# VectorE's order in the late position steps of a Fourier-mixing encoder: lower parts ahead of the late sum and the norm

## The chip, the core and the metric

One NeuronCore of a Trainium2 chip runs the whole program. TensorE (PE in the profile, with its weight loads as PEld) multiplies matrices into PSUM, VectorE (DVE) and ScalarE (ACT) work element by element, GpSimd (POOL) does small things and some transfers, SyncE (SP) issues most transfers. Each engine runs its own instructions strictly in the order in which they were written for it and waits on semaphores for the others. The metric is the device time of one execution in microseconds, the median of several runs.

## The reference

Two sequences (2048 and 512 positions, 1024 channels) pass an attention layer and a Fourier-mixing layer, each with a gate and a residual, and a final RMSNorm. The change lies in the Fourier layer's tail:

```python
def fourier_layer(x, g, w_gate, w_out):
    h = rmsnorm(x, g)
    hg = h.astype(jnp.float32).reshape(b, s, N_FGROUPS, FGROUP_CH)
    f = jnp.fft.fftn(hg, axes=(1, 3), norm="ortho").real
    gate = h @ w_gate
    return x + (f * jax.nn.silu(gate)) @ w_out
# trunk: ... return rmsnorm(x, final_norm)
```

## The kernel before

Float32 products are made of three TensorE products of a high and a lower part ("fp32r"): ScalarE casts a tile to its high part, VectorE subtracts that from the tile to get the lower part, and `matmul3` (L117) issues high x high, high x lower, lower x high. So of every three matmuls the second needs VectorE's lower part.

The transform over the 2048 positions is split by 16: after butterflies on VectorE (`pm`, L1261) there are nine position transforms k1 = 0 to 8. Transform k1 multiplies the tables of sines and cosines with a real and an imaginary tile, in two halves of 512 columns: `halves_of` (L1394) makes the parts, called gp_half_i (i = 0 real, 1 imaginary), and `position` (L1412) the products ABp_0 and ABp_1 (12 + 12 matmuls). VectorE then combines ABp into two row tiles `up` (L1445 to L1448), multiplies them by the gates s2p (L1451), TensorE transposes them (`tw`, L95), and the output product with w_out follows. The transforms come in the order 0, 8, 4, 2, 6 and then, in a loop of **late steps**, 1, 7, 3, 5. The inputs of 7, 3 and 5 are written to DRAM when the butterflies make them (`god`, on ACT's queue, L1824) and read back later (`go`, on SP's queue, L1841). In the text "step 7" is the late step that transforms k1 = 7; while it does so, TensorE also makes the output product of the transform before (k1 = 1).

From transform 6 on the output product is done by `Outs.products` (L1565) with seven 512 x 512 products for two row tiles xa and xb, by sums of operands (a Winograd scheme). In PE's order:

- W = A00 x wo, then VectorE adds W to xa: the **first sum**;
- Z = S1 x T1, then VectorE adds Z to the upper half of xb: the **Z add**. Z is not cleared: the S4 product below accumulates on it, so PE must wait for the Z add;
- ABp_0 of the next transform, W += S2 x T2 (PE must wait for the first sum), ABp_1;
- Z += S4 x wo, then X, half of W += S3 x T3, the transposes `tw`, the other half, the next step's A00, seven matmuls of its Z, then W += A11 x N4 of this step, and the **late sum** (VectorE adds W to the lower half of xb);
- then the **norm** of xb: squares on ScalarE (jkf, L1056), mean (invf, L110), the power on GpSimd (L111), the scaling on VectorE (L1468), a store of the row tile (L1470).

What is late in one step (late sum, norm of xb, third sum S3 and tT_11 of `rest`) is written into the next step, among the parts of the next transform. `seq("dve", ...)` chains VectorE's instructions of these steps in the order in which the Python code calls them, so the code's order is the engine's order; PE's, ACT's and SP's places are left to a scheduler that follows. The hooks are `split_g` (L1849, called after the first sum), `transform` (L1865) and `turns` (L1871). Before, VectorE's order in `split_g` and `transform` is: late sum, first sum, real lower part, mean of the norm, imaginary lower part, S3, tT_11, scaling, Z add, then both lower parts of the second half.

Of the kernel before, what the change touches and what calls it, by code (L numbers as in the profile page):

```python
# [42 lines left out]
def encoder(  # L43
# [120 lines left out]
    def seq(engine, ins):  # L164

        after(ins, chain.get(engine))
        chain[engine] = ins
        return ins
# [822 lines left out]
    def fourier_phase(tail):  # L991
        with ExitStack() as es:
# [401 lines left out]
            def halves_of(name, gr, gs, hf, after_one=None):  # L1394

                out = []
                for i, g in enumerate((gr, gs)):
                    if i and after_one:
                        after_one()
                    if g is not None:  # L1400
                        t = main.tile([P, 2, 512], F32R, align_bytes=LINE, tag="hT", bufs=8, name=f"g{name}_{hf}_{i}")
                        gv = g[:, hf * 512 : hf * 512 + 512]
                        ACT.copy(t[:, 0], gv)
                        low = DVE.tensor_tensor(t[:, 1], gv, f32(t[:, 0]), ALU.subtract)
                        if chain.get("steps"):
                            seq("dve", low)
                        out.append(t)
                return out
# [65 lines left out]
            def normed(x2, r):  # L1474
                norm(x2, r)()
# [8 lines left out]
            def finish(uT, r, between=None):  # L1484
                r0 = r[0]
                x2 = residual(r)
                for half in range(2):
                    if half and between:
                        chain["turns"] = end
                        between()  # L1490
                    ps = psum2.tile([P, 512], F32, tag="acc", name=f"fo{r0}_{half}")
                    for k in range(KD):
                        first_one = k == 0 and half == (between is not None)
                        end = matmul3(
                            ps, uT[k], wo[half * KD + k], k == 0, k == KD - 1, behind=chain.get("turns") if first_one else None
                        )
                    xs = x2[:, half * 512 : half * 512 + 512]
                    DVE.tensor_tensor(xs, xs, ps, ALU.add)
                if between:
                    late[0] = x2, r  # L1500
                else:
                    normed(x2, r)
                return end
# [3 lines left out]
            class Outs:  # L1507
# [57 lines left out]
                def products(self, hooks, last=False):  # L1565
# [5 lines left out]
                    def add(t, half, ps):  # L1571
                        return DVE.tensor_tensor(t[:, q[half]], t[:, q[half]], ps, ALU.add)
# [41 lines left out]
                        upper()  # L1614
                    if not last:
                        prod(W, A[1, 1], ft["N4"], four, False)
                        seq("dve", add(xb, 0, W))
                        return xb, self.us[1][1]
                    ss = main.tile([P, 8], F32, tag="ss", bufs=2, name="ssl")
                    junk = fp.tile([P, 512], F32, tag="c12", bufs=1, name="jkl").bitcast(BF16)  # L1620

# [142 lines left out]
            def pm(a, b, name):  # L1764

                n = zt(name)
                tt(n, a, b, A)
                tt(a, a, b, S)
                return n, a
# [45 lines left out]
            o0s, o1s = pm(tsn[1], tsn[3], "o0s")  # L1815
            g1r, g7r = pm(e0c, o0c, "g1r")
            g1s, g7s = pm(o0s, e0s, "g1s")
            g3r, g5r = pm(e1c, o1s, "g3r")
            p6 = [halves_of("p6", *G[6], 0), None]
            g5s, g3s = pm(o1c, e1s, "g5s")  # L1820
            G[1], G[7], G[3], G[5] = (g1r, g1s), (g7r, g7s), (g3r, g3s), (g5r, g5s)
            for k1 in (7, 3, 5):
# [22 lines left out]
            for k1, k2 in ((1, 7), (7, 3), (3, 5), (5, None)):  # L1845
                name, tiles = f"p{k1}", pair(k1, 16, 0)
                gl, tb = nxt["r"]

                def split_g():  # L1849

                    nxt["s"] = [gated(name, r, place) for r, place in zip(tiles, (xtile, left))]
                    scaled = []

                    def weigh():
                        if late[0]:
                            scaled.append(norm(*late[0], "dve"))

                    nxt["p"] = [halves_of(name, *gl, 0, weigh), None]
                    o.rest()
                    for f in scaled:  # L1860
                        f()
                    if not ft["T3"]:
                        f_sums("T3", right)

                def transform(third):  # L1865
                    if not ft["N4"]:
                        f_sums("N4", left)
                    nxt["p"][1] = halves_of(name, *gl, 1)
                    nxt["o"] = Outs(k1, position(name, k1, *gl, tiles, (nxt["s"], tb), nxt["p"], third))

                def turns():  # L1871
                    nxt["o"].operands()
                    nxt["o"].load()
                    if k2:
                        nxt["r"] = reads(k2)

                late[0] = o.products((split_g, transform, turns, lambda: nxt["o"].others()))
                o = nxt["o"]
            o.products((lambda: (o.rest(), normed(*late[0])), lambda third: third(), lambda: None), last=True)


    fourier_phase(attention_phase())
# [98 lines left out]
```

## Time and profile before

| what | value |
|---|---|
| median of 3 runs | 1584.42 us (1582.39 to 1585.3) |
| the profiled execution | 1583.8 us, of which the profile's span is 1582.0 |
| granted TensorE clock | 0.999 of full speed |
| busy share of the span | PE 99%, PEld 83%, DVE 73%, ACT 56%, POOL 28% |
| transform 6 and late steps 1, 7, 3, 5 | about 1428 to 1561 us of the span |

In the profile a row of the timeline reads: start in us from the span's start, length in us, engine, line, operation, output <- inputs, shape, how many were merged, and in brackets the idle time before it with what ended that. A matmul's length includes its passage through the array, so the next may start before it ends; the distance of two starts is what a matmul costs. VectorE's lengths overlap a little in the same way (a 128x512 subtraction is 0.69 long, and the next instruction starts 0.60 after it).

### The profile page before, as it was taken

How to read it: one execution, taken by the hardware profiler on the slowest of the kernel's cores; microseconds unless marked ns; L12 is line 12 of the kernel's file. 1: busy time of each engine (PE TensorE's matmuls, PEld its weight loads, DVE VectorE, ACT ScalarE, POOL GpSimd, SP SyncE). 2: the span in 40 equal slices, each digit the busy share in tenths (PEclk: the TensorE clock that was granted, in tenths of full speed). 3: DMA queues.
4: the chain of work that ended last, by engine and by line, in shares of the span. 5: the costliest groups of instructions: out<-in, count | busy, mean ns of one | idle time of the engine just before them, and what ended most of it. 6: DMA issues, size and time to landing. Idle time of an engine off the chain costs nothing.

```text
span 1582.0 us, 27728 instructions
## 1 busy us (share of the span) xinstructions
PE 1568.8 (99%) x9882; PEld 1315.8 (83%) x9882; DVE 1151.3 (73%) x2793; ACT 878.1 (56%) x2096; POOL 444.2 (28%) x614
## 2 busy tenths in 40 slices
PE   9999999999999999999999999999999999999998
PEld 7888888888888888988888888888888888887776
DVE  6888556877457886378764577669778878988886
ACT  7788535776246784267751576546555554343343
POOL 2475642421404314024222242223112121111110
PEclk9999999999999999999999999999999999999999
DMA  8597686575856567665659566675557569448752
GB/s 302 205 331 280 227 356 210 210 266 194 303 202 225 207 234 271 214 221 210 251 172 326 205 231 231 236 259 196 191 213 253 180 228 411 171 181 313 278 180 81
DMA packets 100997, 373.91 MB, mean 236 GB/s; under 512 B 11267, under 2 KB 22283, under 8 KB 83452
## 3 DMA queue, kind: packets, MB, share of 16 engines
q1 hardware_dynamic: 83148, 298.17, 52.9%
q0 software_dynamic: 16400, 70.04, 11.4%
q10 hardware_dynamic: 1312, 3.94, 0.7%
q8 instruction: 78, 1.28, 0.3%
q14 instruction: 59, 0.48, 0.1%
HBM read 280.84 MB, written 91.26 MB: 235 GB/s over the span
## 4 chain that ended last, share of the span: by engine, by line
PE 91%; DVE 4%; DMA 2%; ACT 1%; issue 1%; POOL 0%; POOLq 0%; SPq 0%; DVEq 0%; ACTq 0%
PE gp L117 14%; PE qp L117 14%; PE spt L117 11%; PE op L117 7%; PE W L117 7%; PE av L615 6%; PE spt L530 6%; PE fo L117 4%; PE vp L117 3%; PE Z L117 3%; PE pt L589 3%; PE Wo L117 2%; PE z L117 2%; PE X L117 2%; PE ABp L117 1%; PE Zo L117 1%
## 5 line engine op out<-in xcount | busy, mean ns | idle before, releaser
L117 PE MATMUL gp<-h,wg 128*128 128x512 f32 x960 | 237.7, 396 | 0.0
L117 PE MATMUL qp<-h,wq 128*128 128x512 f32 x960 | 237.1, 396 | 0.0
L549 DVE CUSTOM_DVE_ANT_0 S<-spt,b 128x385 f32<-128x385 f32 (+1 forms) x320 | 156.6, 528 | 105.7 <-PE spt L530 68.4
L117 PEld LDWEIGHTS gp<-h,wg 128*128 128x128 f32 x960 | 174.9, 188 | 37.2 <-issue 1.0
L117 PEld LDWEIGHTS qp<-h,wq 128*128 128x128 f32 x960 | 174.9, 188 | 36.6 <-issue 0.2
L557 ACT ACTIVATE S<-S 128x385 f32<-128x385 f32 (+1 forms) x320 | 188.8, 597 | 19.6 <-DVE S L549 19.3
L597 ACT CAST pts<-pt 128x384 fp32r<-128x384 f32 (+1 forms) x240 | 100.5, 457 | 167.6 <-PE pt L589 158.4
L598 DVE TENSOR_TENSOR pts<-pt,pts 128x384 fp32r<-128x384 f32 (+1 forms) x240 | 114.3, 520 | 23.7 <-ACT pts L597 22.7
L117 PE MATMUL spt<-wo,uT 128*128 128x512 f32 x480 | 120.3, 391 | 0.0
L639 POOL TENSOR_TENSOR uT<-o,uT 128x256 fp32r<-128x256 f32 x75 | 55.5, 740 | 229.8 <-ACT uT L638 229.7
L117 PE MATMUL op<-wo,uT 128*128 128x512 f32 x480 | 118.9, 391 | 0.0
L530 PE MATMUL spt<-kwin,qab 64*128 64x384 f32 (+1 forms) x960 | 118.5, 353 | 0.0
L615 PEld LDWEIGHTS av<-pts,v 128*128 128x128 f32 x576 | 101.4, 188 | 18.8
L615 PE MATMUL av<-pts,v 128*128 128x512 f32 (+1 forms) x576 | 115.7, 341 | 0.0
L117 PE MATMUL fo<-wo,tTu 128*128 128x512 f32 x480 | 115.5, 392 | 0.0
L117 PEld LDWEIGHTS op<-wo,uT 128*128 128x128 f32 x480 | 89.4, 188 | 18.5
L117 PEld LDWEIGHTS spt<-wo,uT 128*128 128x128 f32 x480 | 89.1, 188 | 18.3
L117 PEld LDWEIGHTS fo<-wo,tTu 128*128 128x128 f32 x480 | 88.3, 188 | 17.5 <-ACT wo L1722 0.3
L569 DVE TENSOR_SCALAR S<-S 128x384 f32<-128x384 f32 (+1 forms) x192 | 95.8, 499 | 6.8
L530 PEld LDWEIGHTS spt<-kwin,qab 64*128 64x128 f32 x960 | 74.5, 186 | 28.2 <-issue 26.4
L635 POOL TENSOR_TENSOR o<-o,s 128x256 f32<-128x256 f32 x75 | 55.3, 737 | 134.4 <-DVE o L633 134.0
L589 PEld LDWEIGHTS pt<-ident,S 64*128 64x128 f32 x1328 | 78.2, 138 | 4.3 <-issue 2.0
(331 smaller groups left out, 3178.5 us busy)
## 6 DMA issues: line engine op xcount, KB each, us to landing
wo<-wsd SPq DMA_DIRECT2D x32, 1024.0 KB, 4.9
wq<-wsd SPq DMA_DIRECT2D x31, 1024.0 KB, 6.6
wg<-wsd SPq DMA_DIRECT2D x31, 1024.0 KB, 5.3
x<-x1d SPq DMA_DIRECT2D x40, 512.0 KB, 3.5
b<-b21d SPq DMA_DIRECT2D x40, 512.0 KB, 6.6
b<-rowd SPq DMA_DIRECT2D x40, 384.0 KB, 4.3
xs<-in_x_dram SPq DMA_DIRECT2D x23, 512.0 KB, 7.3
s2d<-gt POOLq DMA_DIRECT2D x40, 256.0 KB, 4.7
```

The source lines that it names most:

```text
L117: ins = pe(PE.matmul(out, a[i], b[j], start=start and i + j == 0, stop=stop and i == 1, skip_group_check=more))
L530: pe(PE.matmul(banks[j][:, 2 + k0 * P : 2 + k1 * P], res["q"][rows, qp, b * P : (b + 1) * P], kwin[g][rows, kp, b * P + k0 * P : b * P + k ...
L549: seq(DVE, DVE.tensor_tensor_reduce(out=s[:, e0:e1], in0=ps[:, 1 + e0 : 1 + e1], in1=st["bias"][:, j, 386 - e1 : 386 - e0][:, ::-1], scale ...
L557: last_exp[0] = seq(ACT, ACT.activation(s[:, e0:e1], s[:, e0:e1], AF.Exp, bias=s[:, 386:387], scale=-1.0, accum_out=s[:, 387:388]))
L569: seq(DVE, DVE.tensor_scalar(s[:, ks], s[:, ks], den, None, ALU.mult))
L589: pe(PE.transpose(ps[h][:, kb, j, :], ss[j][rows, 1 + kb * P : 1 + (kb + 1) * P], ident[rows, rows]))
L597: seq(ACT, ACT.copy(hi, ps[:, k0:k1]))
L598: seq(DVE, DVE.tensor_tensor(lo, ps[:, k0:k1], f32(hi), ALU.subtract))
L615: pe(PE.matmul(to, v, pt, start=n == part == 0, stop=part == 1 and n in (1, len(todo) - 1), skip_group_check=n > 1,))
L635: eng.tensor_tensor(o, o, s, ALU.mult)
L639: low = eng.tensor_tensor(lo, o, f32(hi), ALU.subtract)
```

## The change

```diff
@@ Outs.products
                     if not last:
                         prod(W, A[1, 1], ft["N4"], four, False)
-                        seq("dve", add(xb, 0, W))
-                        return xb, self.us[1][1]
+                        return xb, self.us[1][1], lambda: seq("dve", add(xb, 0, W))
@@ finish (the row tile that precedes the late steps)
-                    late[0] = x2, r
+                    late[0] = x2, r, lambda: None
@@ butterflies of the odd transforms
             g1s, g7s = pm(o0s, e0s, "g1s")
-            g3r, g5r = pm(e1c, o1s, "g3r")
             p6 = [halves_of("p6", *G[6], 0), None]
+            g3r, g5r = pm(e1c, o1s, "g3r")
+            p6[1] = halves_of("p6", *G[6], 1)
             g5s, g3s = pm(o1c, e1s, "g5s")
@@ the late steps
                 def split_g():
                     nxt["s"] = [gated(name, r, place) for r, place in zip(tiles, (xtile, left))]
-                    scaled = []
-
-                    def weigh():
-                        if late[0]:
-                            scaled.append(norm(*late[0], "dve"))
-
-                    nxt["p"] = [halves_of(name, *gl, 0, weigh), None]
-                    o.rest()
-                    for f in scaled:
-                        f()
+                    xb, r, whole = late[0]
+                    nxt["p"] = [halves_of(name, *gl, 0, whole)]
+                    o.halve(3)
+                    scaled = norm(xb, r, "dve")
+                    o.own(1, 1)
+                    nxt["p"].append(halves_of(name, *gl, 1))
+                    scaled()
@@
                 def transform(third):
-                    nxt["p"][1] = halves_of(name, *gl, 1)
@@ the last products
-            o.products((lambda: (o.rest(), normed(*late[0])), lambda third: third(), lambda: None), last=True)
+            def old():
+                xb, r, whole = late[0]
+                whole()
+                o.rest()
+                normed(xb, r)
+
+            o.products((old, lambda third: third(), lambda: None), last=True)
```

No instruction is added or taken away. The late sum is called from within `halves_of`, between the real and the imaginary lower part, so the first sum and the real lower part stand ahead of it. The norm's mean stands behind S3, and its scaling behind both lower parts of the second half. For transform 6 the first half's parts are called one butterfly pair sooner, and the second half's parts ahead of the last pair.

Three places show what moves. First VectorE in late step 3, from the instruction after tT7_01 to the Z add. In the names, x2_15 is the old xb, x2_7 and x2_9 the new xa and xb, gp3 the parts of transform 3, invf15 the norm's mean of row tile 15, and Wo1, Wo7, Zo7 the PSUM tiles of the products of transforms 1 and 7. Before:

```order
L1572 TENSOR_TENSOR x2_15_16906<-x2_15_16906,Wo1_16950 128x512
L1572 TENSOR_TENSOR x2_7_17147<-x2_7_17147,Wo7_17193 128x512
L1404 TENSOR_TENSOR gp3_0_0_17212<-go3_0_17151,gp3_0_0_17212 128x512
L110 TENSOR_SCALAR invf15_17218<-ssf15_17215 128x1
L1404 TENSOR_TENSOR gp3_0_1_17221<-go3_1_17152,gp3_0_1_17221 128x512
L1015 TENSOR_TENSOR S3_7_17224<-F3_7_17137,S3_7_17224 128x512
L1524 TENSOR_TENSOR tT7_11_17227<-tw1_17113,tT7_11_17227 128x512
L1468 SCALAR_TENSOR_TENSOR x2_15_16906<-x2_15_16906,invf15_17218,gfb_15159 128x1024
L1572 TENSOR_TENSOR x2_9_17149<-x2_9_17149,Zo7_17194 128x512
L1404 TENSOR_TENSOR gp3_1_0_17245<-go3_0_17151,gp3_1_0_17245 128x512
L1404 TENSOR_TENSOR gp3_1_1_17248<-go3_1_17152,gp3_1_1_17248 128x512
```

and with the change:

```order
L1572 TENSOR_TENSOR x2_7_17147<-x2_7_17147,Wo7_17192 128x512
L1404 TENSOR_TENSOR gp3_0_0_17211<-go3_0_17151,gp3_0_0_17211 128x512
L1572 TENSOR_TENSOR x2_15_16906<-x2_15_16906,Wo1_16949 128x512
L1404 TENSOR_TENSOR gp3_0_1_17215<-go3_1_17152,gp3_0_1_17215 128x512
L1015 TENSOR_TENSOR S3_7_17218<-F3_7_17137,S3_7_17218 128x512
L110 TENSOR_SCALAR invf15_17224<-ssf15_17221 128x1
L1524 TENSOR_TENSOR tT7_11_17227<-tw1_17113,tT7_11_17227 128x512
L1404 TENSOR_TENSOR gp3_1_0_17230<-go3_0_17151,gp3_1_0_17230 128x512
L1404 TENSOR_TENSOR gp3_1_1_17233<-go3_1_17152,gp3_1_1_17233 128x512
L1468 SCALAR_TENSOR_TENSOR x2_15_16906<-x2_15_16906,invf15_17224,gfb_15159 128x1024
L1572 TENSOR_TENSOR x2_9_17149<-x2_9_17149,Zo7_17193 128x512
```

The same eleven instructions: the first sum and gp3_0_0 pass the late sum, gp3_0_1 and S3 pass the mean, gp3_1_0 and gp3_1_1 pass the scaling and the Z add.

Second, PE at the same place, where the products of transform 3's first half meet the product S2 x T2 of transform 7. Before:

```order
L117 MATMUL Zo7_17194<-fT1_3_16502,S1_7_17140 128x512 x3
L117 MATMUL ABp3_0_17253<-gp3_0_0_17212,tbp3_17157 128x260
L117 MATMUL Wo7_17193<-fT2_0_16504,S2_7_17143 128x512 x3
L117 MATMUL ABp3_0_17253<-gp3_0_0_17212,tbp3_17157 128x260 x2
L117 MATMUL ABp3_0_17253<-gp3_0_1_17221,tbp3_17157 128x260
L117 MATMUL Wo7_17193<-fT2_1_16506,S2_7_17143 128x512
L117 MATMUL ABp3_0_17253<-gp3_0_1_17221,tbp3_17157 128x260 x2
```

and with the change:

```order
L117 MATMUL Zo7_17193<-fT1_3_16502,S1_7_17140 128x512 x3
L117 MATMUL ABp3_0_17253<-gp3_0_0_17211,tbp3_17157 128x260 x3
L117 MATMUL ABp3_0_17253<-gp3_0_1_17215,tbp3_17157 128x260
L117 MATMUL Wo7_17192<-fT2_0_16504,S2_7_17143 128x512 x2
L117 MATMUL ABp3_0_17253<-gp3_0_1_17215,tbp3_17157 128x260 x2
```

PE asks for the real lower part at once, without three matmuls of W in between, and for the imaginary one after two of them instead of after four and three of the real part.

Third, VectorE ahead of transform 6. gp6 are its parts, g3r, od0_0 (which becomes the real input of transform 5), g5s and tc1 the butterflies whose results are stored to `god`, x2_12 the row tile that is scaled there:

```order
 L1261 TENSOR_TENSOR g1s_16421<-o0s_16415,e0s_16412 128x1024
-L1261 TENSOR_TENSOR g3r_16424<-od0_0_16146,od1_1_16152 128x1024
+L1404 TENSOR_TENSOR gp6_0_0_16424<-ev0_1_15654,gp6_0_0_16424 128x512
 L1261 TENSOR_TENSOR o0s_16415<-o0s_16415,e0s_16412 128x1024
 L110 TENSOR_SCALAR invf12_16401<-ssf12_16398 128x1
+L1404 TENSOR_TENSOR gp6_0_1_16427<-ev2_1_15658,gp6_0_1_16427 128x512
+L1468 SCALAR_TENSOR_TENSOR x2_12_16344<-x2_12_16344,invf12_16401,gfb_15159 128x1024
+L1261 TENSOR_TENSOR g3r_16430<-od0_0_16146,od1_1_16152 128x1024
+L1404 TENSOR_TENSOR gp6_1_0_16433<-ev0_1_15654,gp6_1_0_16433 128x512
 L1261 TENSOR_TENSOR od0_0_16146<-od0_0_16146,od1_1_16152 128x1024
```

The lower parts go forward past g3r and od0_0, and those two go back past the scaling and three lower parts; their stores to `god` follow them on ACT's queue. PE's order follows there too: the second matmul of transform 6 now stands after 11 matmuls of the product fo2_0 and not after 32 of fo2_0 and fo2_1.

More of the change, by code (lines that the diff above doesn't have):

```diff
@@ L1817, in fourier_phase @@
             g1s, g7s = pm(o0s, e0s, "g1s")
+            p6 = [halves_of("p6", *G[6], 0), None]
             g3r, g5r = pm(e1c, o1s, "g3r")
-            p6 = [halves_of("p6", *G[6], 0), None]
+            p6[1] = halves_of("p6", *G[6], 1)
             g5s, g3s = pm(o1c, e1s, "g5s")
```

## Prediction

> **What bounds the kernel now.** I read the page's head first, then the chain of waits in order of time, then the timelines of PE, VectorE and ScalarE from 1425 us on, where the change lies. The head:
>
> ```profile
> PE 1568.8 (99%) x9882; PEld 1315.8 (83%) x9882; DVE 1151.3 (73%) x2793; ACT 878.1 (56%) x2096; POOL 444.2 (28%) x614
> PE 91%; DVE 4%; DMA 2%; ACT 1%; issue 1%; POOL 0%; POOLq 0%; SPq 0%; DVEq 0%; ACTq 0%
> ```
>
> PE carries the chain. An order change gains only what PE waits in these steps, and loses what it makes PE wait anew. How large the waits are must be read from starts, since a matmul's length holds its passage through the array. Step 1 is nearly free of waits after its first products and gives the price:
>
> ```profile
> 1463.46 2.91 PE L117 MATMUL Wo<-fT,S 128*128 128x512 f32 x12
> 1466.21 1.62 PE L117 MATMUL ABp<-gp,tbp 128*128 128x260 f32 x12
> 1467.67 2.90 PE L117 MATMUL Zo<-wo,S 128*128 128x512 f32 x12
> ```
>
> Twelve products of W take 1466.21 - 1463.46 = 2.75 (0.229 each), twelve ABp 1.46 (0.122 each). So the stretch from the first ABp_0 to the S4 product of Z, 24 ABp and 12 W, costs 2 x 1.46 + 2.75 = 5.67 without waits; I take 5.75, for the change of kind in the middle. In steps 7, 3 and 5 it runs:
>
> ```profile
> 1485.39 0.28 PE L117 MATMUL ABp<-gp,tbp 128*128 128x260 f32 x1
> 1488.47 1.23 PE L117 MATMUL ABp<-gp,tbp 128*128 128x260 f32 x8 [1.12 <-DVE gp L1404]
> 1492.07 1.82 PE L117 MATMUL ABp<-gp,tbp 128*128 128x260 f32 x11 [0.41 <-DVE gp L1404]
> 1493.73 2.91 PE L117 MATMUL Zo<-wo,S 128*128 128x512 f32 x12
> ...
> 1511.46 0.28 PE L117 MATMUL ABp<-gp,tbp 128*128 128x260 f32 x1
> 1516.88 1.83 PE L117 MATMUL ABp<-gp,tbp 128*128 128x260 f32 x11 [0.42 <-DVE gp L1404]
> 1518.55 2.90 PE L117 MATMUL Zo<-wo,S 128*128 128x512 f32 x12
> ...
> 1536.27 0.28 PE L117 MATMUL ABp<-gp,tbp 128*128 128x260 f32 x1
> 1543.36 2.91 PE L117 MATMUL Zo<-wo,S 128*128 128x512 f32 x12
> ```
>
> Step 7 takes 8.34, steps 3 and 5 take 7.09 each. Over 5.75 that is 2.59, 1.34 and 1.34: all that can be had there, 5.27 together. The rows name VectorE's lower parts (gp, L1404) as what ends the waits.
>
> **The late steps, part by part.** What holds the lower parts back in step 7:
>
> ```profile
> 1482.99 0.68 DVE L1524 TENSOR_TENSOR tT<-tw,tT 128x512 fp32r<-128x512 f32 x1
> 1484.46 1.28 DVE L1572 TENSOR_TENSOR x<-x,Wo 128x512 f32<-128x512 f32 x2 [0.78 <-PE Wo L117]
> 1487.66 0.15 DVE L110 TENSOR_SCALAR invf<-ssf 128x1 f32<-128x1 f32 x1 [1.32 <-ACT jkf L1056]
> 1490.73 0.68 DVE L1572 TENSOR_TENSOR x<-x,Zo 128x512 f32<-128x512 f32 x1
> 1483.26 1.27 ACT L1403 CAST gp<-go 128x512 fp32r<-128x512 f32 x2 [1.74 <-DMA go<-god]
> 1486.48 1.06 ACT L1056 ACTIVATE jkf<-x 128x1024 bf16<-128x1024 f32 x1
> ```
>
> VectorE is free at 1483.6, waits 0.78 for PE's N4 product because the late sum stands first, and then 1.32 for ScalarE's square because the mean stands ahead of the imaginary lower part. With the change the first sum and the real lower part run in the 0.78 (1483.6 to 1484.8 at 0.60 each; the cast of that part is done near 1483.9), the late sum follows at 1484.8 and the imaginary part at 1485.4, ready some 0.74 later, at 1486.14. PE reaches its real lower part at 1485.39 + 0.12 and its imaginary one after four ABp and two W, at 1485.39 + 4 x 0.122 + 2 x 0.229 = 1486.3. Neither waits. S3 ends at 1486.6, and the mean still waits for the same square (1486.48, behind four casts on ScalarE) until 1487.66. Behind it are tT_11 and the second half's parts (1487.73 to 1489.5); PE wants them from 1485.39 + 1.46 + 2.75 = 1489.6 on: in time.
>
> What is late next is the **Z add**. Between the mean and it stand, before, the imaginary part, S3, tT_11 and the scaling, and now tT_11, two lower parts and the scaling: the same four lengths. So it stays at 1490.73 and ends near 1491.41, and PE, which now comes to S4 at 1485.39 + 5.75 = 1491.14, waits about 0.33 for it. Step 7 gains 2.59 - 0.33 = **2.26**.
>
> In steps 3 and 5 the square is not held up:
>
> ```profile
> 1510.52 1.28 DVE L1572 TENSOR_TENSOR x<-x,Wo 128x512 f32<-128x512 f32 x2 [0.77 <-PE Wo L117]
> 1512.48 0.15 DVE L110 TENSOR_SCALAR invf<-ssf 128x1 f32<-128x1 f32 x1
> ```
>
> The late sum moves from 1510.52 to 1510.87 (after the first sum and one part from 1509.66), the square and the mean by the same 0.35, to 1512.83. Then tT_11 and two parts (1.8), scaling (1.2), Z add at 1515.9 until 1516.58; PE wants Z at 1511.46 + 5.75 = 1517.2, 0.6 later. GpSimd's power hides behind the 1.8. So steps 3 and 5 gain 1.34 each, **2.68**. The scaling, and with it the store of xb and the loads queued behind it on SP, comes about 0.3 later in the step; those loads are wanted some 15 us later and cost nothing. The transposes still find their up tiles:
>
> ```profile
> 1522.31 1.22 DVE L1451 TENSOR_TENSOR up<-up,s2p 128x1024 f32<-128x1024 f32 x1
> 1525.46 1.21 PE L95 MATMUL tw<-ident,up 64*128 64x64 f32 x32
> ```
>
> The last up ends at 1523.5, 1.9 ahead. VectorE's work between the Z add and it is the same and starts from a Z add 0.36 later than now with two parts (1.2) less behind it, so it ends 0.8 sooner, while PE comes 1.34 sooner: 1.4 of the 1.9 is left. In step 7 the Z add does not move: up 1.2 sooner, PE 2.26, 0.9 left.
>
> At the very end two products of the last N4 are now pulled between the last Z and W:
>
> ```profile
> 1561.08 0.40 PE L117 MATMUL Vo<-fN,tT 128*128 128x256 f32 x2
> 1561.49 3.01 PE L117 MATMUL Wo<-fT,S 128*128 128x512 f32 x12
> ```
>
> They cost 0.41 for two at 0.12; the change puts them with the other 22. Gain 0.41 - 0.24 = **0.17**.
>
> **Transform 6 and step 1.** Here PE waits for VectorE once, and step 1 then waits for a transfer:
>
> ```profile
> 1428.36 7.46 PE L117 MATMUL fo<-wo,tTu 128*128 128x512 f32 x32
> 1436.48 0.63 PE L117 MATMUL ABp<-gp,tbp 128*128 128x260 f32 x3 [0.66 <-DVE gp L1404]
> 1430.54 1.22 DVE L1261 TENSOR_TENSOR g3r<-od,od 128x1024 f32<-128x1024 f32 x1
> 1434.53 1.28 DVE L1468 SCALAR_TENSOR_TENSOR x<-x,invf,gfb 128x1024 f32<-128x1024 f32 x1 [0.44 <-POOL invf L111]
> 1449.69 10.61 DMA x<-x1d
> 1460.39 0.69 DVE x L1572
> 1461.08 0.60 DVE gp L1404
> 1461.76 0.60 PE ABp L117 x3
> ```
>
> The real lower part takes g3r's place at 1430.54 and is ready at 1431.3; PE, whose order moved too, wants it after eleven products, at 1428.36 + 11 x 0.229 = 1430.9: a wait of 0.4. With o0s, the mean, one part, the scaling (1.72 behind the mean, as now) and g3r ahead, the second half's real part starts near 1436.3 and is ready at 1437.1; PE wants it at 1436.2: 0.9. Together 1.3 for 0.66 and 0.2 hidden in the starts: PE comes to step 1 up to 0.45 later. That costs nothing as long as step 1 begins with a wait for the residual tile x of row 6, which lands at 1460.39 and holds VectorE's first sum and the lower part behind it. PE's first ABp there stood at 1460.72 and waited till 1461.76; gone that cover, it costs the 0.45.
>
> So what this part costs is what it does to that load. Its bytes come in a full queue:
>
> ```profile
> 1438.00:1439.00 1.00, 1.00 (x7) 0.72 (x6) 1.00 (x3) 0.38 (x1) 0.00 (x0) 1.00 0.00 0
> 1450.00:1464.00 14.00, 13.23 (x63) 10.75 (x62) 9.91 (x17) 7.72 (x15) 0.95 (x2) 1.00 1.01 390
> god<-tc ACTq DMA_DIRECT2D x1, 512.0 KB, 7.6
> fT<-fT2d SPq DMA_DIRECT2D x4, 512.0 KB, 10.8
> SPq L1667 <- DMA god<-tc: 4.1, 1, 4.1
> ```
>
> The last two columns of the windows are DMA share and GB/s. The DMA is idle in the microsecond from 1438 and busy all the time around the load (share 1.01, 390 GB/s). A store of 512 KB costs 0.524 MB / 390 GB/s = 1.3 there. The change moves g3r's store by some 5 us and od's by 4 (from about 1434 to 1438): g3r's still falls before the full stretch, od's half into the idle microsecond and half beyond. I take **-0.7** for the landing of x, and with it for everything behind. The ends: +0.5 if the load follows its issue (the scaling of row 2 ahead of it on SP ends perhaps that much sooner), -2.6 if both stores fall wholly into the full stretch.
>
> **Sum.** 2.26 + 2.68 + 0.17 - 0.7 = 4.4. The profiled execution took 1583.8 (span 1582.0 and 1.8 around it): 1579.4. It lies 0.6 below the median of 1584.42, so I forecast a median of **1580.0**. One bound more: in step 7 the parts of `go` land at 1483.26, late; if DMA's load shifts less than PE there, the 0.33 goes too.
>
> **The rivals.** About 0.2% (3.2 us: below 1581.25, above 1587.6) is what a measurement of this kernel tells from no change.
>
> *The load of row 6 does not feel the moved stores* (the share shows gaps before 1439 that could take both): 4.4 + 0.7 = 5.1, so 1579.3. Chance 0.13.
>
> *Step 7 is held by its transfer, not by the norm's place.* For: the cast waits 1.74 for `go`. Against: the cast of the imaginary part is done by 1484.5, three microseconds ahead of its subtraction. If the wait of 1.12 stays, step 7 gains 1.14: 3.3 in all, 1581.1. Chance 0.12.
>
> *Only the named waits go.* PE's idle time by its busy row is 1.12 + 0.41 in step 7 and 0.4 each in steps 3 and 5, 2.35 in all; if that is all that PE loses, the result is 2.35 - 0.7 = 1.7, so 1582.7. For it speaks the busy share of 99%; against it the 5.67 of step 1, made of the same matmuls. Chance 0.11. [...]
>
> *Slower: the stores hold up the residual load.* Row 2's store, and behind it on SP the load of row 6, now waits for the store of tc to land, which starts near 1441.1 (before 1439.9). SP's wait of 4.1 shows that such a landing does hold SP. With 7.6 it lands at 1448.7 and costs nothing; if it takes as long as the slowest of the loads issued around it,
>
> ```profile
> DMA to landing us min/median/max: 4.7/7.5/12.2
> ```
>
> it lands at 1453.3, the load is issued at 1453.8 instead of 1449.69, and with 12.2 of its own it lands at 1466.0, 5.6 late: 5.1 - 5.6 = -0.5, so 1584.9. From 5.1 us of delay on the change loses, and each more costs one; a mean landing of transfers that waited twice as long would give 1590. For it: the queue is full. Against: tc's store took 7.6 beside fT2 loads of 10.8. Chance 0.09. [...]
>
> That the order does not come out as written is no rival: the instructions stand as the code says.
>
> **How the numbers follow.** The forecast has 0.55 (about 0.45 of it below 1581.25), the others 0.13, 0.12, 0.11 and 0.09. Faster: 0.45 + 0.12 + 0.06 = 0.63. Slower: most of the last rival's worse end and a little for what no row shows, 0.07. Same: 0.30. The runs before scatter by 1.5 to each side of their middle; the range from 1577.3 (5.9 gained with step 7's 0.33 and the load's +0.5, less scatter) to 1583.6 holds all but the slower cases and a part of the third rival's scatter.
>
> **What would show it.** Right: in steps 7, 3 and 5 the first ABp_0 to the S4 product takes about 6.1, 5.75 and 5.75; no PE wait on gp there; in step 7 a short wait before S4 for the Z add; x of row 6 landing at 1460 to 1462; the square in step 7 still behind four casts. Wrong: a PE wait for gp after the first two W, a Z add later than S4 in steps 3 and 5, `tw` waiting for up, or a landing of row 6's x beyond 1463.

## The result and the profile after

| | before | changed |
|---|---|---|
| median of 15 runs each | 1583.36 us (1582.06 to 1585.3) | 1579.9 us (1578.73 to 1581.81) |
| ratio | | 0.9979, 95% interval 0.9972 to 0.9985 |
| span of the profile | 1582.0 us | 1577.4 us, granted clock 0.998 |

The change makes the kernel 0.21% faster, 3.5 us by the medians. The median before is lower here than the 1584.42 of the three runs from which the forecast was made.

The page after, in its busy line and its shares of the chain of waits, shows the same number of instructions on every engine, and PE busy for 2.7 us less. What PE no longer waits for is read from the timeline below it.

```profile
PE 1566.1 (99%) x9882; PEld 1316.2 (83%) x9882; DVE 1151.1 (73%) x2793; ACT 878.4 (56%) x2096; POOL 443.2 (28%) x614
PE 92%; DVE 4%; DMA 2%; issue 1%; ACT 1%; POOL 0%; SPq 0%; ACTq 0%; POOLq 0%; DVEq 0%
```

PE's timeline after, from transform 6 on, with the rows that answer to those of before:

```profile
1428.32 0.41 PE L117 MATMUL ABp<-gp,tbp 128*128 128x260 f32 x2
1431.48 0.63 PE L117 MATMUL ABp<-gp,tbp 128*128 128x260 f32 x3 [0.22 <-DVE gp L1404]
1436.74 0.63 PE L117 MATMUL ABp<-gp,tbp 128*128 128x260 f32 x3 [0.17 <-DVE gp L1404]
...
1460.90 0.28 PE L117 MATMUL ABp<-gp,tbp 128*128 128x260 f32 x1
1462.93 1.83 PE L117 MATMUL ABp<-gp,tbp 128*128 128x260 f32 x11 [1.75 <-DVE gp L1404]
1468.79 2.91 PE L117 MATMUL Zo<-wo,S 128*128 128x512 f32 x12
...
1486.51 0.65 PE L117 MATMUL ABp<-gp,tbp 128*128 128x260 f32 x4
1492.16 2.99 PE L117 MATMUL Zo<-wo,S 128*128 128x512 f32 x12
...
1509.97 0.65 PE L117 MATMUL ABp<-gp,tbp 128*128 128x260 f32 x4
1515.62 2.91 PE L117 MATMUL Zo<-wo,S 128*128 128x512 f32 x12
...
1533.35 0.65 PE L117 MATMUL ABp<-gp,tbp 128*128 128x260 f32 x4
1539.00 2.91 PE L117 MATMUL Zo<-wo,S 128*128 128x512 f32 x12
...
1567.61 3.03 PE L117 MATMUL Vo<-fN,tT 128*128 128x256 f32 x24
```

From the first ABp_0 to the S4 product of Z steps 7, 3 and 5 now take 5.65 each (1492.16 - 1486.51 and so on), and no row between carries a wait: that is the unstalled stretch. Step 1 went the other way: its eleven ABp start 2.03 after the first one, where it was 1.02 before (1461.74 - 1460.72).

VectorE's timeline after, step 1's first sum and step 7, and the two ScalarE rows that it waits on:

```profile
1461.58 0.69 DVE L1572 TENSOR_TENSOR x<-x,Wo 128x512 f32<-128x512 f32 x1 [4.47 <-DMA x<-x1d]
...
1488.35 0.15 DVE L110 TENSOR_SCALAR invf<-ssf 128x1 f32<-128x1 f32 x1 [0.55 <-ACT jkf L1056]
1489.02 1.28 DVE L1404 TENSOR_TENSOR gp<-go,gp 128x512 fp32r<-128x512 f32 x2
1491.42 0.68 DVE L1572 TENSOR_TENSOR x<-x,Zo 128x512 f32<-128x512 f32 x1
```

```profile
1483.99 1.24 ACT L1403 CAST gp<-go 128x512 fp32r<-128x512 f32 x2 [1.34 <-DMA go<-god]
1487.17 1.06 ACT L1056 ACTIVATE jkf<-x 128x1024 bf16<-128x1024 f32 x1
```

The mean still waits for the square, and the square still stands behind four casts, but nothing that PE wants stands behind the mean any more. The Z add ends (1491.42 + 0.68) as PE comes to S4 (1492.16).

### The profile page after: what moved, and what is told of

It is laid out like the page before. It is cut to its first block, busy times and chain, and to the rows that moved or that the text cites. A ratio compares the mean times of both kernels' runs of the same rounds, so it can differ in the third digit from the quotient of the medians.

```text
span 1577.4 us, 27736 instructions
## 1 busy us (share of the span) xinstructions
PE 1566.1 (99%) x9882; PEld 1316.2 (83%) x9882; DVE 1151.1 (73%) x2793; ACT 878.4 (56%) x2096; POOL 443.2 (28%) x614
## 4 chain that ended last, share of the span: by engine, by line
PE 92%; DVE 4%; DMA 2%; issue 1%; ACT 1%; POOL 0%; SPq 0%; ACTq 0%; POOLq 0%; DVEq 0%
PE gp L117 14%; PE qp L117 14%; PE spt L117 11%; PE op L117 7%; PE W L117 7%; PE av L615 6%; PE spt L530 6%; PE fo L117 4%; PE vp L117 3%; PE Z L117 3%; PE Wo L117 3%; PE pt L589 3%; PE z L117 2%; PE X L117 2%; PE Zo L117 2%; PE ABp L117 1%
```

## The experiments

Two executions reach transform 6 at times that differ by up to 1.8 us (1427.81 to 1429.65 in the profiles here), for reasons that lie ahead of the change and were not looked into. So the profiles are compared by a **count**: from the start of the first two ABp of transform 6 to the end of the last Vo. For the changed kernel it is 1567.61 + 3.03 - 1428.32 = 142.32. "x6" is the start of step 1's first sum, which waits for the residual tile of row 6, on the same scale (1461.58 - 1428.32 = 33.26). Each row of the table is worked out in this way from one profile; the ratio is to the kernel before, run on the same chip.

| kernel | x6 | step 1 | step 7 | 3 | 5 | count | ratio (95% interval) |
|---|---|---|---|---|---|---|---|
| before, first profile | 32.27 | 6.95 | 8.34 | 7.09 | 7.09 | 147.17 | 1 |
| before, second profile | 32.25 | 6.94 | 7.11 | 7.09 | 7.10 | 145.92 | |
| changed, first profile | 33.26 | 7.89 | 5.65 | 5.65 | 5.65 | 142.32 | 0.9979 (0.9972 to 0.9985) |
| changed, second profile | 33.29 | 7.88 | 5.67 | 5.65 | 5.65 | 142.28 | |
| e1 late steps only | 32.27 | 6.87 | 5.65 | 5.66 | 5.65 | 141.25 | 0.9967 (0.9955 to 0.9979) |
| e2 sixth transform only | 33.22 | 9.45 | 7.10 | 7.09 | 7.10 | 148.46 | 1.0007 (0.9998 to 1.0016) |
| e3 late sum only | 32.28 | 6.95 | 7.56 | 7.49 | 7.48 | 146.88 | 1.0006 (0.9997 to 1.0015) |
| e4 norm and parts, sum between | 32.27 | 6.89 | 5.81 | 5.81 | 5.82 | 141.74 | 0.9971 (0.9960 to 0.9981) |
| e5 e1, parts behind the scaling | 32.28 | 7.18 | 7.80 | 6.52 | 6.52 | 145.36 | 0.9984 (0.9975 to 0.9993) |
| e6 e1, load ahead | 30.09 | 5.64 | 5.65 | 5.66 | 5.66 | 139.95 | 0.9962 (0.9949 to 0.9976) |
| e7 change, g5s first | 33.05 | 9.24 | 5.65 | 5.64 | 5.65 | 143.59 | 0.9977 (0.9968 to 0.9986) |
| e8 change, load ahead | 30.77 | 5.63 | 5.65 | 5.65 | 5.67 | 140.02 | 0.9964 (0.9952 to 0.9976) |
| e9 sum first, norm behind | 32.28 | 6.89 | 6.04 | 6.04 | 6.04 | 142.75 | 0.9981 (0.9972 to 0.9990) |

(A step's number is its stretch from the first ABp_0 to the S4 product of Z. All times are in us.)

### e1 and e2: the two parts of the change apart

e1 is the changed kernel with the sixth transform's lines put back; e2 is the kernel before with the same lines moved.

```diff
@@ e1, against the changed kernel (e2: the reverse, against the kernel before)
-            p6 = [halves_of("p6", *G[6], 0), None]
             g3r, g5r = pm(e1c, o1s, "g3r")
-            p6[1] = halves_of("p6", *G[6], 1)
+            p6 = [halves_of("p6", *G[6], 0), None]
```

e1, as expected:

> The changed kernel with the sixth transform's lower parts put back to their old place; the late steps stay changed. Theory A (the two parts of the change act through the load of row 6's residual tile alone): the tile lands as before, near 1460.4 instead of 1461.6, so PE's eleven ABp of step 1 start near 1461.75 and not 1462.93, 1.1 us sooner. In step 7 the go parts do not move by as much, so PE comes to S4 about 0.3 before the Z add and step 7's stretch takes 5.9 to 6.0 instead of 5.65. Span 1576.5 to 1576.8, 0.6 to 0.9 below the changed kernel's 1577.4; ratio to before about 0.9966. Rival B (the late landing came by chance, the move of the lower parts is free): landing scatters, span within 0.3 of 1577.4. Rival C (the old place costs PE its 0.66 of waiting in transform 6 again, and that reaches the end): span 0.4 or more above 1577.4.

e2, as expected:

> The kernel before with nothing but the sixth transform's lower parts moved ahead of g3r's pair and of od. Theory A: tile of row 6 lands near 1461.6, step 1 loses 1.1; in step 7 the go parts move by 0.7 and VectorE's old order waits for them, so about 0.4 of it is given back: span 1582.6 to 1583.1 against 1582.0, ratio 1.0004 to 1.0008. Rival B (the move is free): landing near 1460.4, ratio 0.9997 to 1.0002. Rival C (it gains PE's wait in transform 6): ratio 0.9995 or less.

x6 is 32.25 to 32.28 in all seven profiles with the old place and 33.22 to 33.29 in the three with the new one, whatever the late steps do: the move costs about 1.0 in the landing, not by chance, and B falls in both. e1's count is 1.07 below the changed kernel's, and its ratio is the lower of the two, though the intervals overlap. So by the counts the late steps alone would have been the better change. Two parts of the expectation missed. The span, 1577.1, lies above the range, as this execution reaches transform 6 0.75 later than the changed kernel's (1429.07 for 1428.32). And e1's step 7 has no wait for the Z add, since go's parts landed early in that execution (its square starts 0.33 after the first ABp_0, in the changed kernel's profile 0.66). C falls too: the 0.65 of PE's wait in transform 6 is there again in e1, and step 1 begins at 32.60 in the count, as in the changed kernel (32.58).

e2 is slower than before by as much as expected, though its interval just holds 1. Its profile loses another 1.6 in step 1. The windows of e2, with the granted clock in the third column from the right, show why:

```profile
1463.00:1464.50 1.50, 0.86 (x5) 0.65 (x5) 1.50 (x4) 0.00 (x0) 0.73 (x1) 1.00 0.91 330
1464.50:1467.50 3.00, 3.00 (x12) 2.71 (x12) 3.00 (x5) 0.38 (x1) 0.14 (x1) 0.50 0.80 325
1468.00:1471.00 3.00, 3.00 (x20) 2.67 (x19) 1.57 (x4) 0.01 (x1) 0.00 (x0) 1.00 1.01 315
```

Right behind step 1's wait PE ran at half its clock for three microseconds. That is no property of the order (the changed kernel's two profiles have the same wait at clock 1.00), and is taken up at the end.

### The kernel before once more: what step 7's length was

> The kernel before, unchanged, profiled once more. Counted from the first two ABp of transform 6 to the end of the last Vo, the first profile of it took 147.2 us. Theory E (the long step 7 of that profile, 8.34 from its first ABp_0 to S4 beside 7.09 in steps 3 and 5, is an accident of that execution: its go parts landed late): the cast of go begins 2.5 or more ahead of the step's first ABp_0 (it was 2.13), step 7 takes 7.1 to 7.3, and the whole count about 146.0. Theory F (it belongs to the order): step 7 takes 8.2 or more and the count is 147 again.

E holds. PE's row of the step's start and of S4, then ScalarE's of go's cast and of the square, in the second profile of the kernel before:

```profile
1485.18 0.28 PE L117 MATMUL ABp<-gp,tbp 128*128 128x260 f32 x1
1492.29 2.90 PE L117 MATMUL Zo<-wo,S 128*128 128x512 f32 x12
```

```profile
1481.62 1.23 ACT L1403 CAST gp<-go 128x512 fp32r<-128x512 f32 x2 [0.30 <-DMA go<-god]
1485.03 1.06 ACT L1056 ACTIVATE jkf<-x 128x1024 bf16<-128x1024 f32 x1
```

The cast comes 3.56 ahead of the first ABp_0 where it came 2.13 ahead in the first profile, the square stands 0.15 ahead of it and not 1.09 behind, and the step takes 7.11. So 1.23 of the 8.34 was the late landing of `go` in that one execution. e5 has it again: its cast waits 2.19 for `go`, and its step 7 takes 7.80 beside 6.52 in the others. In the changed kernel's first profile the cast comes later still in the count (1483.99 - 1428.32 = 55.67; before 1483.26 - 1428.12 = 55.14 and 1481.62 - 1427.94 = 53.68), and its step 7 takes 5.65. So with the new order a landing as late as that no longer reaches PE. Why `go` lands up to 1.5 apart between executions was not tried.

### e3, e4, e5, e9: which piece of the late steps does it

In all four the sixth transform is as before. e3 moves the late sum alone; e5 is e1 with the second half's parts at their old place; e4 and e9 keep the norm and the parts as in the change and differ in the late sum. The diffs below are against the changed kernel and do not show all of the removed lines; e3 has the line in `transform` that is named at e5 as well.

```diff
@@ e3, split_g
+                    def weigh():
+                        whole()
+                        scaled.append(norm(xb, r, "dve"))
+                    nxt["p"] = [halves_of(name, *gl, 0, weigh), None]
+                    o.rest()
+                    scaled[0]()
@@ e4, split_g
                     xb, r, whole = late[0]
+                    whole()
-                    nxt["p"] = [halves_of(name, *gl, 0, whole)]
+                    nxt["p"] = [halves_of(name, *gl, 0)]
@@ e9, Outs.products
-                        return xb, self.us[1][1], lambda: seq("dve", add(xb, 0, W))
+                        seq("dve", add(xb, 0, W))
+                        return xb, self.us[1][1], lambda: None
@@ e5, split_g (and in transform: nxt["p"][1] = halves_of(name, *gl, 1))
-                    nxt["p"].append(halves_of(name, *gl, 1))
                     scaled()
```

> Late steps with the late sum behind the first sum and the real lower part, but the norm's mean still ahead of the imaginary part and the second half's lower parts still behind the scaling and the Z add; sixth transform as before. Theory A (the mean and the place of the second half's parts are what hold the step, the 0.78 us of VectorE's wait for PE is spare time as long as they stand there): no gain in step 7 (second half's parts still wanted from 1489.6 and there at 1492.0), steps 3 and 5 slower by up to 0.35 each since the square follows the sum, tail gains 0.3: span 1582.0 to 1582.4, ratio 0.9999 to 1.0003. Rival D (each wait that goes is gained): 0.78 in each of three steps, span 1579.7, ratio 0.9985.

> Late steps with the late sum first, as before, but the norm behind the lower parts and the second half's lower parts ahead of the scaling; sixth transform as before. Theory A: the real lower part is ready 0.85 later than PE wants it in each late step (1486.35 against 1485.51), and PE's order puts only one product of W into that time; nothing else is late. Step 7's stretch 6.3 to 6.5, steps 3 and 5 6.2 to 6.5: gains 1.9, 0.7 and 0.7, tail 0.3: span 1578.2 to 1578.8, ratio 0.9977 to 0.9982. Rival D (each wait that goes is gained by itself): the mean's 1.32 in step 7 and little in steps 3 and 5, span 1580.3 or more, ratio 0.9989 or more.

> e1 (late steps changed, sixth transform as before) with one piece put back: the second half's lower parts stand behind the scaling and the Z add again. Theory A (that place is a third cause, worth something by itself): the parts are ready 1.2 + 0.6 = 1.8 later than now, some 0.3 to 0.5 after PE wants them, so the stretch of each late step takes 6.0 to 6.2 instead of 5.65; 1.0 to 1.5 in all: span near 1578.3, ratio 0.9973 to 0.9977. Rival G (the twelve products of W cover it): 5.65, ratio 0.9967 as e1. Rival H (PE stands as long as before the change): 7.1, ratio 0.9995.

> e4 with the late sum really at its old place, ahead of the first sum (in e4 it stood behind the first sum, which already fills VectorE's wait): norm and second half's lower parts behind as in the change, sixth transform as before. Theory A (the late sum's place costs little once the norm is behind, since PE's order puts three products of W into the gap): the real lower part comes 0.6 later than in e4, two more products of W cover 0.46 of it, so each late step takes 5.85 to 6.05 instead of e4's 5.81 and the change's 5.65; count to the end 141.9 to 142.5, ratio 0.9972 to 0.9977. Rival D (the 0.78 us of VectorE's wait is all PE's loss): 6.4 and more a step, count 143.5, ratio 0.9983.

e3 loses 0.4 in each late step. VectorE and PE of e3 in step 3:

```profile
1512.23 0.15 DVE L110 TENSOR_SCALAR invf<-ssf 128x1 f32<-128x1 f32 x1 [1.27 <-ACT jkf L1056]
1515.90 1.29 DVE L1404 TENSOR_TENSOR gp<-go,gp 128x512 fp32r<-128x512 f32 x2
```

```profile
1510.82 0.65 PE L117 MATMUL ABp<-gp,tbp 128*128 128x260 f32 x4
1516.64 1.83 PE L117 MATMUL ABp<-gp,tbp 128*128 128x260 f32 x11 [1.29 <-DVE gp L1404]
1518.31 2.91 PE L117 MATMUL Zo<-wo,S 128*128 128x512 f32 x12
```

VectorE's wait of 0.78 for PE is gone, and a longer one, 1.27, stands in front of the mean: the square follows the late sum, the scaling and the Z add follow the mean, and the second half's parts, which PE wants, follow them all. Theory A's sign holds and D falls. The loss is a little larger than expected, 0.40 for 0.35 in steps 3 and 5, and step 7, held against the 7.11 of the second profile, loses 0.45. The tail gives 0.3 back, which leaves 0.96 by the counts. By the medians e3 is 0.9 slower than before, but its interval holds 1.

e4 was meant to have the late sum first. But in the code the first sum is added before `split_g` runs, so e4's late sum stands between the first sum and the real lower part, and the first sum fills VectorE's wait. That leaves 0.16 a step. e9 has it really first, with the wait of 0.78 back, and takes 6.04: 0.39 a step over the change. VectorE's row of the two sums in e9's step 7, then PE's rows of that step:

```profile
1484.10 1.28 DVE L1572 TENSOR_TENSOR x<-x,Wo 128x512 f32<-128x512 f32 x2 [0.78 <-PE Wo L117]
```

```profile
1485.04 0.28 PE L117 MATMUL ABp<-gp,tbp 128*128 128x260 f32 x1
1485.44 0.96 PE L117 MATMUL Wo<-fT,S 128*128 128x512 f32 x3
1486.24 0.54 PE L117 MATMUL ABp<-gp,tbp 128*128 128x260 f32 x3
1491.08 2.91 PE L117 MATMUL Zo<-wo,S 128*128 128x512 f32 x12
```

PE's order puts three products of W into the gap. So e4's misses (0.16 a step where 0.6 to 0.8 was expected, a ratio of 0.9971 for 0.9977 or more) have two reasons: its late sum was not first, and even a first one costs only 0.39. e9's step came as expected; its count (142.75 for at most 142.5) and its ratio (0.9981 for at most 0.9977) did not, because its tail is the old one again: from step 5's S4 to the end it takes 31.94, as before, where the changed kernel and the other experiments with a moved late sum take 31.61 to 31.64.

e5 shows the third piece. PE of e5 in step 3:

```profile
1511.71 0.65 PE L117 MATMUL ABp<-gp,tbp 128*128 128x260 f32 x4
1516.57 1.83 PE L117 MATMUL ABp<-gp,tbp 128*128 128x260 f32 x11 [0.37 <-DVE gp L1404]
1518.23 2.91 PE L117 MATMUL Zo<-wo,S 128*128 128x512 f32 x12
```

6.52, so 0.87 a step, more than the 0.3 to 0.5 expected: from 1516.57 to S4 PE takes 1.66 for eleven ABp that cost 11 x 0.122 = 1.34, so behind the named wait for the real part it waits for the imaginary one as well.

For a step of 7.09 to 7.10 before, the pieces therefore do not add. The sum alone gives -0.4; with the norm behind it, but the parts where they were, the step falls to 6.52; with the norm and the parts moved, but the sum first, to 6.04; with all to 5.65.

### e6 and e8: the load of row 6 taken out of the way

The last two loads of fT2 go behind the residual loads of rows 6 and 10 in SP's queue; e6 does it on e1, e8 on the changed kernel.

```diff
-            f_sums("T2", right)
+            f_sums("T2", right, (0, 1))
             finish(*pend.pop(0))
             finish(*pend.pop(0), o.operands)
             o.others()
             o.load()
+            f_sums("T2", right, (2, 3))
```

> e1 with the last two loads of fT2 issued behind the residual loads of rows 6 and 10 instead of ahead of row 2's store. Theory A (step 1 waits for row 6's tile because 1 MB of fT2 stands ahead of it in the queue, 2.7 us at 390 GB/s): the tile lands some 30.0 after the first ABp of transform 6 instead of 32.3, step 1's wait of 1.0 goes, the two fT2 loads land before W's third product wants them. Gain 0.5 to 1.0 over e1, the lower end if go's parts, which are not moved by as much, then bound step 7: span 1576.0 to 1576.6, ratio 0.9960 to 0.9964. Rival I (fT2's last two are late now): a wait inside W of step 1, nothing gained or up to 1.5 lost, ratio 0.9967 to 0.9977.

> The changed kernel whole, sixth transform moved too, with the last two loads of fT2 behind the residual loads of rows 6 and 10 as in e6. Theory A (the move of the sixth transform's parts costs through row 6's tile alone, and gains nothing, since PE begins step 1 no sooner for it): the tile lands near 31.0 after the first ABp of transform 6, ahead of the 32.7 at which step 1 wants it, so the cost of 1.0 is gone; first ABp of transform 6 to the end 139.9 as in e6, ratio 0.9962 as e6. Rival J (the cost has a second way, by row 2's store or go's parts): 140.7 or more, ratio 0.9967. Rival K (PE's shorter waits in transform 6, 0.39 for 0.66, are a gain once the tile is early): 139.6, ratio 0.9960.

SP, then PE of e6:

```profile
1450.81 0.91 SPq L1479 DMA_DIRECT2D x<-x1d  x2
1451.77 1.01 SPq L1666 DMA_DIRECT2D fT<-fT2d  x2
```

```profile
1461.83 1.61 PE L117 MATMUL ABp<-gp,tbp 128*128 128x260 f32 x12
1463.28 2.91 PE L117 MATMUL Wo<-fT,S 128*128 128x512 f32 x12
1466.02 1.61 PE L117 MATMUL ABp<-gp,tbp 128*128 128x260 f32 x12
1467.47 2.91 PE L117 MATMUL Zo<-wo,S 128*128 128x512 f32 x12
```

The tile is there before PE, and step 1 takes 5.64, the unstalled stretch. e8 reaches the same count with the sixth transform moved (140.02 beside 139.95): its cost is gone, so it went by way of row 6's tile alone, and no gain shows in its place. J and K fall. The move still shows in x6, 30.77 for 30.09, but now ahead of PE. e6 and e8 have the lowest times of all, 1577.34 and 1577.3 by their medians, some 2.3 below the changed kernel by the counts; their intervals lie below 1 and overlap that of the changed kernel.

### e7 and the changed kernel once more

```diff
@@ e7, against the changed kernel
             g3r, g5r = pm(e1c, o1s, "g3r")
-            p6[1] = halves_of("p6", *G[6], 1)
             g5s, g3s = pm(o1c, e1s, "g5s")
+            p6[1] = halves_of("p6", *G[6], 1)
```

> The changed kernel with the second half's lower parts of the sixth transform behind g5s and tc: g3r and its store stay late as in the change (about 4.3 later than before), od's too, but g5s and tc come 1 earlier than in the change's order and no later than before. Theory M (row 6's tile lands late because the loads of fT2 wait for the stores of g5s and tc, which the change moved back by 1.2, and the DMA stands idle for that time): the tile lands at 32.3 or less after the first ABp of transform 6, as before. Theory N (as predicted: it lands late because the bytes of g3r's and od's stores fall into the full stretch): 33.2 as in the change. Span 1576.8 to 1577.3 by M, 1577.4 or more by N; ratio 0.9967 against 0.9977.

> The changed kernel, profiled once more. If the account by terms holds: 5.65 in each late step, row 6's tile 33.2 to 33.3 after the first ABp of transform 6 (32.25 before), count to the end 142.3, that is 3.6 below the second profile of the kernel before (145.92). A longer step 1 (9.2) would mean that the lower clock seen there in e2 and e7 comes with the long wait in some executions.

With fT2's loads issued early (12.75 after transform 6's first ABp; 12.88 before, 14.92 in the changed kernel), e7's tile still lands at 33.05. M falls. The case is not clean, since row 2's scaling came later too and the load was issued 2.2 later than before (23.74 in the count for 21.57); but a load issued 2.2 later that lands 0.8 later speaks for bytes, not for the issue, and the bytes counted below say the same. e7's profile has the half clock of e2 in its step 1; its ratio is that of the changed kernel.

The second profile of the changed kernel repeats the first to 0.04 in the count, at full clock.

## Why the prediction held, step by step

**The whole.** Forecast 1580.0, measured 1579.9. But the working gave 4.4 and the medians give 3.5: two errors met, and that the times agree to 0.1 is luck. The base, 1584.42, was 1.06 above the median of 15 runs. And step 7's term was 0.8 too large, while the misses of the other terms cancel.

**Step 7, 2.26 predicted.** Between the two first profiles it gave 2.69 (8.34 to 5.65). Between the second profiles it gave 1.44 (7.11 to 5.67), the same as in steps 3 and 5. This is the step that failed: the working took the 8.34 of one execution for a property of the order. The mechanism named (mean behind a square behind four casts) was right for that execution; what delayed the casts was the landing of `go`, which the cast row's wait of 1.74 showed. The rival that step 7 is held by that transfer had this right of the kernel before, and wrong of the changed one, where the norm no longer stands in front. Of the 0.33 of waiting for the Z add (the working's own ends, 1491.41 and 1491.14, differ by 0.27) at most 0.09 came, for the reason given as a bound: go's cast moved by 0.73 (1483.26 to 1483.99) and PE by 1.12.

**Steps 3 and 5, 1.34 each.** 1.44 and 1.44. The stretch is 5.65, not 5.75: the allowance for the change of kind was not needed, step 1's 5.67 was the price.

**The tail, 0.17.** 0.30, from step 5's S4 to the end (31.64 for 31.94). The two early Vo had also held the W behind them (1561.49 to 1564.34 is 2.85, now 2.72). The gain hangs on the late sum's move: every profile with the sum moved has it, e9 with the sum at its old place and e2 (31.95) do not.

**Row 6's load, -0.7.** -0.95 (step 1 7.89 for 6.94). The sign and the mechanism held, the size was off (and g3r and od moved back by 4.1 and 3.5 in the count, not by 5 and 4). The windows from 1.88 to 12.88 after transform 6's first ABp, of before and of the changed kernel (the last two columns are DMA share and GB/s):

```profile
1430.00:1441.00 11.00, 10.34 (x53) 8.35 (x52) 10.56 (x13) 1.27 (x4) 1.40 (x1) 1.00 0.75 276
```

```profile
1430.20:1441.20 11.00, 10.61 (x56) 8.39 (x55) 10.56 (x13) 1.54 (x5) 0.86 (x1) 1.00 0.66 228
```

The DMA is idle for 0.09 x 11 = 1.0 us more while it still has room, and has moved 48 x 11 = 528 KB less, the size of one store. The prediction let g3r's store fall ahead of the full stretch and only half of od's beyond; the work lost there is a whole store's worth, and the tile lands 1.0 later.

That it is the bytes, and not the later issue, can be counted. From transform 6's first ABp to x6 the DMA moves 10.9 MB in the kernel before (32.27 us at 338 GB/s), in the changed kernel (33.26 at 328), in e2 (33.22 at 329) and in e7 (33.05 at 330), while the load of row 6 is issued at 21.57, 21.92, 22.20 and 23.74 in the count. The tile is there when the same bytes are through, whenever it was asked for within these 2.2 us.

Row 2's store did wait for tc's landing, as the slower rival said (SP's waits in the changed kernel from 1436 to 1486: us in all, times, the longest):

```profile
SPq L1470 <- DMA god<-tc: 1.6, 1, 1.6
```

But tc took 8.4 where that rival needed 12.2 or more, and the load was issued only 0.35 later in the count (1450.24 - 1428.32 beside 1449.69 - 1428.12).

**Transform 6.** PE waits 0.22 and 0.17 where 0.4 and 0.9 were expected; hidden all the same, as said. Step 1 begins at 32.58 in the count, before at 32.60.

**The sum by the profiles without the accident** (before's second and the changed kernel's first): step 1 -0.95, steps 7, 3 and 5 +1.46, +1.44, +1.45, the tail +0.30, and -0.09 behind step 7, where the S4 product took a little longer (2.99 for 2.91; the Z add ends just as PE comes there, so this may be what is left of that wait): 3.61, and the counts differ by 145.92 - 142.32 = 3.60. The medians say 3.5.

**The rivals.** That the load does not feel the stores fell by e1 and e2. That only the named waits go (2.35) fell by the 4.35 that the three steps gave. The slower one was seen at work, at a fifteenth of its threshold (0.35 of 5.1, and 0.10 of that is the scaling, which came later).

## What to carry to other kernels

On a chain of ordered instructions, price the pieces of a reordering together: here the piece that removed a visible wait lost time alone and paid only once the norm had left its place in front of the parts that the busiest engine wants. Before a stretch of one profile is taken as the price of an order, hold it against its sisters in the same profile; the one that is longer by more than they differ among themselves may be an accident of a transfer. And ask of every moved store whether it leaves a stretch in which the DMA had nothing else to do.

## What the runs showed of the hardware

**Behind PE waits of 1.69 and 1.53 us the granted clock was 0.50 for about 3.4 us; behind three others of 1.55 to 1.75 it was not.** Five of the 13 profiles have a PE wait of more than 1.5 us from 1425 us on: step 1 of the changed kernel (idle 1.75 and 1.74 in its two profiles), of e2 (1.69) and of e7 (1.53), and step 7 of e5 (1.55). Behind it e2 and e7 ran at a granted clock of 0.50 for about 3.4 us (in windows of half a microsecond e2 has 0.53 in the one from 1464.5, 0.50 in the five that follow and 0.56 in the one from 1467.5; e7 has 0.65 in the one from 1465.0, 0.50 in the six that follow and 0.94 in the one from 1468.5); the other three show 1.00 in every window there. The window of e7, with the granted clock again in the third column from the right:

```profile
1465.50:1468.50 3.00, 3.00 (x9) 2.42 (x9) 3.00 (x5) 0.44 (x2) 0.22 (x1) 0.50 0.92 374
```

From the eleven ABp behind the wait to S4 step 1 takes 7.48 in e2 and 7.42 in e7, where it takes 5.93 in the kernel before and 5.86 in the changed one: the half clock cost 1.55 and 1.56. Behind the next longest wait (1.32, in step 7 of e3) every window shows 1.00. Between 1424 and 1515 us no other microsecond of the 13 profiles has a granted clock below 0.99, and in the first profiles of the two kernels none has one below 0.99 from the start to 1572 us. Why two of the five waits were followed by the half clock and three were not, no run here shows.

**GpSimd's power of one column took 0.55 us with VectorE idle and up to 1.46 beside VectorE's work on two SBUF tiles.** The power in the norm of row 2, first before, with VectorE idle beside it:

```profile
1447.36 0.55 POOL L111 TENSOR_TENSOR invf<-invf,mhalf 128x1 f32<-128x1 f32 x1 [12.86 <-DVE invf L110]
```

Then in the changed kernel, where the mean moved ahead of the second gate product, VectorE's product and the power:

```profile
1446.58 1.23 DVE L1451 TENSOR_TENSOR up<-up,s2p 128x1024 f32<-128x1024 f32 x1
```

```profile
1446.75 1.46 POOL L111 TENSOR_TENSOR invf<-invf,mhalf 128x1 f32<-128x1 f32 x1 [13.12 <-DVE invf L110]
```

It ends 0.4 after VectorE's product of two tiles has ended, so the mean that came 0.8 sooner in the count brought the scaling no sooner (1448.24 - 1428.32 = 19.92, before 19.82). In the first profiles of the two kernels the thirty powers from 1390 us on fall into three groups: 0.55 to 0.57 with VectorE idle or reading a PSUM tile, 0.86 and 0.87 beside a 128x512 subtraction of two SBUF tiles, and 1.40 and 1.46 beside a 128x1024 operation on two SBUF tiles.
